# Loading and splitting the second up unit ahead of a norm chain, two small copies on another engine, and one head's transposes a matmul group sooner

## The chip, the cores and the metric

The kernel runs one decoder layer on 1 core of one Trainium2 chip. The metric is the device time of one execution in microseconds: 770.14 us, the median of three runs (770.01 to 772.16).

The core has five instruction streams. PE multiplies matrices into PSUM (PEld is its weight load). DVE (VectorE), ACT (ScalarE) and POOL (GpSimd) work on tiles, and SP (SyncE) only issues transfers; ACT issues transfers too, between its own instructions. Each stream runs in its own order, and an instruction that waits holds up everything behind it on its stream.

## The reference

One layer, 512 positions of width 1024, float32 throughout:

```python
mod = silu(c) @ ada_w + ada_b
sh1, sc1, g1, sh2, sc2, g2 = split(mod, 6)
u = rms_norm(x, mix_pre_g) * (1 + sc1) + sh1
qk, v, o_pre, gates, glu = split(u @ w_in)
h = mlstm(silu(conv4(qk)), v, gates)              # 4 heads of 256, chunks of 128
h = rms_norm(h, ml_norm_g) * sigmoid(o_pre)
y = silu(layer_norm(conv31(a * sigmoid(gt))))     # a, gt = halves of glu
x = x + g1 * rms_norm(concat(h, y) @ w_out, mix_post_g)
u = rms_norm(x, ffn_pre_g) * (1 + sc2) + sh2      # the "second norm"
a, gt = split(conv3(u @ ffn_up))                  # 2 x 2816 columns
x = x + g2 * rms_norm((silu(gt) * a) @ ffn_down, ffn_post_g)
```

## The kernel before

**Precision by splitting.** A large product is made of three fp32r passes. Each weight tile of 128x512 is split: ACT writes the rounded part `h` (`w_split`, L191), and DVE or POOL writes the rest `l` (L192). `mm3` (L210) multiplies h by h, h by l and l by h. A 1 MB weight load gives four such pairs, `_0`, `_512`, `_1024` and `_1536`. It lands in one of two raw buffers (pool `raws`), so a load can be issued only when the last split of the load before the previous one is done.

**Order.** PE and SP run in the order in which the code is written. DVE, ACT and POOL are ordered by a scheduler, except inside `in_order()`, where they too follow the written order. Transfers that ACT issues are placed among its instructions by the scheduler.

**Third head.** For heads 0 to 3, `attention(h)` is a generator that emits scores (`s`, L551), values (`o`, L562), the scaling of `hn` (L587) and last the transposes `hT` (L593) with their splits `hh` (ACT, L599) and `hl` (DVE, L600). While head 2 finishes, `make_vo(3)` emits four groups of 24 matmuls (`vo`), one for each 128 positions. The pair of PSUM banks tagged `at` holds `s`, `o`, `hT` and later `xT` in turn. After head 2, PE emits `ry_s` (L216), the sums of the convolution's layer norm, and head 3's first scores.

**The mixer's end and the second norm.** The output projection has two column halves. `mixa` is done first; `mixb` (four tiles of 128 positions) follows in two parts: eight row blocks for all tiles, then `mix_last(tt, ...)`, the other eight blocks tile by tile. As soon as `mixb` of a tile stands, its chain runs:

- `chain_sums`: square sum (ACT L717), `un = mixb * g1r` (DVE L968), factor `rm` (DVE L724, POOL L726);
- `chain_x`: the new residual `x1` (DVE L975), its square sums (ACT L717), `un = x1 * gs2r` (DVE L978), factor `rf`;
- `chain_u`: `un * rf + sh2r` (DVE L983);
- `turn_tile`: eight transposes on PE into `xT` (L991, the `at` banks); `turn_out`: the split into `u2h` (ACT L998) and `u2l` (DVE L999), which frees the banks.

`gs2r` and `sh2r` are rows spread over all partitions: DVE and ACT make `gains` (L948 to L950), PE transposes them (`gT`), DVE copies `gTs` (L694), SP sends that to DRAM (L696) and reads it back as four broadcasts (L702).

**Up units.** The first up unit (`wup0`) is loaded and split before the chain. Units 1 and 2 are loaded by `raw_up` (L1008) and split by `up_split`, four calls each, at places written into the chain. `up_half(th, i)` multiplies unit i with half of the positions; the first three units run in halves, so that PE starts on tiles 0 and 1 while tiles 2 and 3 are still in the chain. From unit 3 on, all positions are there. `x1` is stored to DRAM (`x1_d`) for the end of the layer.

Of the kernel before, what the change touches and what calls it, by code (L numbers as in the profile page):

```python
# [13 lines left out]
AF = mybir.ActivationFunctionType  # L14
ALU = mybir.AluOpType
# [5 lines left out]
KT = D // P  # L21
NT = T // P
# [33 lines left out]
def decoder_layer(ctx, tc, w_glu0, x, c, adaT, vecs, w_glu, w_qko, w_v0, w_vo, w_out, w_up, w_down, out):  # L56
    nc = tc.nc
    V, S, G, PE = nc.vector, nc.scalar, nc.gpsimd, nc.tensor

    const = ctx.enter_context(tc.tile_pool(name="const", bufs=1))  # L60
    slots = ctx.enter_context(tc.tile_pool(name="slots", bufs=SLOTS))
# [38 lines left out]
    def mmbank(name):  # L100
        return psum.tile([P, T], F32, tag="mm", bufs=4, name=name)

    def atbank(name):
        return psum.tile([P, T], F32, tag="at", bufs=2, name=name)
# [45 lines left out]
    def vcols(name, i, n):  # L150
        a = VEC[name][0] + i
        return vec[:, a : a + n]
# [32 lines left out]
    def w_split(src, name, pool=None, tag="w", eng=None):  # L185

        n = src.shape[1]
        pool = pool or wpool
        hi = pool.tile([P, T], F32R, tag=tag, name=f"{name}h")
        lo = pool.tile([P, T], F32R, tag=tag, name=f"{name}l")  # L190
        S.activation(hi[:, :n], src, AF.Copy)  # L191
        (eng or G).tensor_tensor(out=lo[:, :n], in0=src, in1=hi[:, :n].bitcast(F32), op=ALU.subtract)  # L192
        return hi, lo

    def w_load(view, name, pool=None, tag="w", eng=None):

        n = view.shape[1]
        r = raws.tile([P, 2048], F32, tag="raw", name=name)
        nc.sync.dma_start(r[:, :n], view)
        return [w_split(r[:, a : min(a + T, n)], f"{name}_{a}", pool, tag, eng) for a in range(0, n, T)]  # L200
# [37 lines left out]
    RD = float(D) ** 0.5  # L238
# [35 lines left out]
    for tt in range(NT):  # L274
# [9 lines left out]
        if tt < NT - 1:  # L284
# [7 lines left out]
                    op0=ALU.add)  # L292
# [9 lines left out]
    def u_tiles(name):  # L302
        hi = upool.tile([P, KT, T], F32R, tag="uh", name=f"{name}h")
        lo = upool.tile([P, KT, T], F32R, tag="ul", name=f"{name}l")
        return hi, lo, [(hi[:, j, :], lo[:, j, :]) for j in range(KT)]

    _, _, u = u_tiles("u")
# [211 lines left out]
    def head_load(h):  # L519
        pieces = []  # L520
        for part in range(2 if h else 3):
            pieces += w_load(w_qko[(2 * h + 1 if h else 0) + part], f"wqko{h}_{part}")
        heads[h] = (pieces, [], [], [])

    def head_proj(h, i):

        pieces, qs, ks, so = heads[h]
        ps = mmbank(f"qko{h}_{i}")
        proj(ps, pieces, i * KT)
        e = 2 * h + i % 2  # L530
        if i < 2:
            qs.append(conv4(ps, e, f"q{h}_{i}"))
        elif i < 4:
            ks.append(conv4(ps, 8 + e, f"k{h}_{i}"))
        else:
            t = slot(f"so{h}_{i}")
            S.activation(t, ps, AF.Tanh, scale=0.5)
            so.append(t)
# [146 lines left out]
    RD = float(D) ** 0.5  # L685
    gains = const.tile([P, 4 * KT], F32, name="gains")
    rows_d = [dram.tile([D], F32, tag=f"row{i}", name=f"row_d{i}") for i in range(4)]

    def send_rows(a, n, queue=nc.scalar):

        ps = mmbank(f"gT{a}") if a == KT else atbank(f"gT{a}")
        PE.transpose(ps[:n, :P], gains[:, a : a + n], ident)
        t = (side if a == 3 * KT else slot)(f"gTs{a}")[:, :P]
        V.tensor_copy(t[:n, :], ps[:n, :P])  # L694
        for i in range(n // KT):
            queue.dma_start(rows_d[a // KT + i].rearrange("(j p) -> j p", p=P), t[i * KT : (i + 1) * KT, :])  # L696
# [13 lines left out]
    x1_d = [[dram.tile([P, T], F32, tag=f"x1d{tt}_{hf}", name=f"x1d{tt}_{hf}") for hf in range(2)] for tt in range(NT)]  # L710
# [23 lines left out]
    sc2 = mod[:, 24:40].rearrange("p (j two) -> p j two", two=2)  # L734
# [74 lines left out]
    def pace():  # L809
        tc.cur_priority += LATER  # L810
        next(paced, None)
        tc.cur_priority -= LATER
# [14 lines left out]
    def norm_sums():  # L827
        yr.append(colsum(ysq, T, "ry_s", cvbank))
# [14 lines left out]
    for h in range(H - 1):  # L843
        head_load(h + 1)
        steps = attention(h)
        if h == 0:
            head_proj(1, 0)
            next(steps)
            head_proj(1, 1)
            pace()  # L850
            next(steps)
            pace()
            head_proj(1, 2)
            pace()
            next(steps)
        else:
            next(steps)
            head_proj(h + 1, 0)
            pace()
            for _ in turns:  # L860
                pass
            head_proj(h + 1, 1)
            pace()
            next(steps)
            scaled = last_e[0]
            pace()
            head_proj(h + 1, 2)
            pace()
            next(steps)
        head_proj(h + 1, 3)  # L870
        values = make_vo(h + 1)
        pace()
        next(steps)
        pace()
        next(values)
        next(steps)
        pace()
        next(values)
        if h == 0:
            next(steps)  # L880
            pace()
        make_E(h + 1)
        if h == H - 2:
            norm_mean()
        next(values)
        next(values)
        if h < H - 2:
            turns = steps
        else:
            for _ in steps:  # L890
                pass
        if h == H - 2:
            norm_sums()

# [40 lines left out]
    x1 = side_parts("x1_0") + side_parts("x1_1")  # L935
    x1 = [x1[2 * tt : 2 * tt + 2] for tt in range(NT)]
# [9 lines left out]
        for tt, ps in enumerate(banks):  # L946
            mm3(ps, (hy[k][0][:, tok(tt)], hy[k][1][:, tok(tt)]), wo[n_ % 4], n_ == 0, False)
    V.scalar_tensor_tensor(out=gains[:, KT : 2 * KT], in0=sc2[:, :, 0], scalar=1.0, in1=vcols("ffn_pre_g", 0, KT), op0=ALU.add, op1=ALU.mult)  # L948
    S.activation(gains[:, 2 * KT : 3 * KT], sc2[:, :, 1], AF.Copy)
    S.activation(gains[:, KT : 2 * KT], gains[:, KT : 2 * KT], AF.Copy, scale=RD)  # L950
    wo = [w for g in range(KA // 4, 4) for w in wo_rows(1, g)]
    for tt in range(NT):
        for hf in range(2):
# [8 lines left out]
    def chain_sums(tt):  # L962

        ps = banks[tt]
        sq_sum(ps, msq[:, 2 * tt + 1 : 2 * tt + 2], f"mixb{tt}")
        un = adas.tile([P, D], F32, tag="ada", name=f"un{tt}")
        uns[tt] = [un[:, :T], un[:, T:]]
        V.tensor_tensor(out=uns[tt][1], in0=ps, in1=g1r[1], op=ALU.mult)  # L968
        return token_factor(msq[:, 2 * tt : 2 * tt + 2], f"rm{tt}")
# [31 lines left out]
    def mix_last(tt, a, b):  # L1001
        for n_, k in enumerate(MIX[KA:]):
            if a <= n_ < b:
                mm3(banks[tt], (hy[k][0][:, tok(tt)], hy[k][1][:, tok(tt)]), wo[n_], False, n_ == 2 * KT - KA - 1)

    def raw_up(i):
        r = raws.tile([P, 2048], F32, tag="raw", name=f"wup{i}")
        nc.sync.dma_start(r, w_up[i])  # L1008
        up_w[i] = []
        return r  # L1010

    def up_split(i, r, pool, tag):
        q = len(up_w[i])
        up_w[i].append(w_split(r[:, q * T : (q + 1) * T], f"wup{i}_{q * T}", pool, tag, V))
# [9 lines left out]
                mm3(ps[:, th * HT : (th + 1) * HT], blk(up_w[i], half * KT + k), (u2h[:, th, k, :], u2l[:, th, k, :]), k == 0, k == KT - 1)  # L1024

    up_w = {0: w_load(w_up[0], "wup0", slots, "t", V)}
    send_rows(KT, 2 * KT, nc.sync)
    gs2r = row(1, cvtile, "gs2", nc.sync)
    sh2r = row(2, cvtile, "sh2", nc.sync)
    raw1 = raw_up(1)  # L1030
    raw2 = raw_up(2)
    early += [[mmbank(f"up{i}_{half}") for half in range(2)] for i in range(2)]
    with in_order():
        for tt in range(3):
            mix_last(tt, 0, 2 * KT - KA)
        r = chain_sums(0)
        r = chain_x(0, r)
        up_split(1, raw1, slots, "t")
        chain_u(0, r)
        turn_tile(0)  # L1040
        mix_last(3, 0, 7)
        r = chain_sums(1)
        up_split(1, raw1, slots, "t")
        r = chain_x(1, r)
        up_split(1, raw1, slots, "t")
        chain_u(1, r)
        turn_out(0)
        turn_tile(1)
        mix_last(3, 7, 2 * KT - KA)
        r = chain_sums(2)  # L1050
        turn_out(1)
        r = chain_x(2, r)
        up_split(1, raw1, slots, "t")
        chain_u(2, r)
        up_half(0, 0)
        turn_tile(2)
        r = chain_sums(3)
        up_split(2, raw2, wpool, "w")
        r = chain_x(3, r)
        up_split(2, raw2, wpool, "w")  # L1060
        chain_u(3, r)
        up_half(0, 1)
        up_split(2, raw2, wpool, "w")
        early.append([cvbank(f"up2_{half}") for half in range(2)])
        up_half(0, 2, 0)
        turn_tile(3)
        turn_out(2)
        up_split(2, raw2, wpool, "w")
        turn_out(3)
    up_half(0, 2, 1)  # L1070
    for i in range(NE):
        up_half(1, i)
    for tt in range(NT):
        for hf in range(2):
            nc.scalar.dma_start(x1_d[tt][hf], x1[tt][hf])


    def halves(z):
# [293 lines left out]
```

## Time and profile before

| | before |
|---|---|
| median of three runs | 770.14 us |
| the profiled execution's own time | 771.9 us |
| its span, first to last instruction | 770.2 us |
| PE busy | 758.1 us, 98% |
| DVE / POOL / ACT busy | 575.3 / 522.8 / 407.4 us |
| HBM read / written | 126.59 / 20.07 MB |
| granted PE clock | full speed until the last 21 us |

Times within the trace are counted from the span's first instruction. A row of the timeline gives start, duration, engine, line, operation, the tile written and the tiles read, and, in brackets, how long the engine had been idle and what ended that. The last ends of merged matmul rows are modelled, so the distance from start to start says more than the duration: 128x512 matmuls follow each other at 0.23 us here.

### The profile page before, as it was taken

What the parts mean: (1) busy time and instruction counts of PE and PEld (TensorE: products, weight loads), DVE (VectorE), ACT (ScalarE), POOL (GpSimd) and SP (SyncE); (2) the same over time, 40 slices, a digit from 0 to 9 for tenths busy, and PEclk for the clock granted to TensorE, in tenths of its full rate; (3) what the DMA queues carried; (4) which work ended last, traced back from release to release, by engine and by line L of the source; (5) the groups of instructions that cost most, each with busy time, mean ns of one, the idle gap of its engine ahead of it and who ended that gap; (6) DMA issues with size and microseconds to landing.
All of it is one profiled execution on the core that took longest, in us unless ns stands there. A gap on an engine that the chain in (4) does not pass through costs nothing.

```text
span 770.2 us, 10269 instructions
## 1 busy us (share of the span) xinstructions
PE 758.1 (98%) x3552; PEld 629.9 (82%) x3552; DVE 575.3 (75%) x831; ACT 407.4 (53%) x780; POOL 522.8 (68%) x432
## 2 busy tenths in 40 slices
PE   8999999999999999999998999999999999999996
PEld 6888898878788788788887998888888888888885
DVE  6769999979889686577949798665776578754548
ACT  6685538585665555563334554434444345566633
POOL 4789849794594871645521467876988786699934
PEclk9999999999999999999999999999999999999999
DMA  8973214311131350656953655756586683896273
GB/s 315 365 266 134 86 56 149 125 55 55 55 114 52 110 212 8 246 191 200 371 188 108 251 181 207 283 214 240 193 300 222 224 296 145 316 398 243 95 235 148
DMA packets 40138, 147.34 MB, mean 191 GB/s; under 512 B 3827, under 2 KB 5267, under 8 KB 30485
## 3 DMA queue, kind: packets, MB, share of 16 engines
q1 hardware_dynamic: 26372, 94.50, 34.2%
q10 hardware_dynamic: 13712, 52.18, 18.8%
q8 instruction: 28, 0.46, 0.2%
q14 instruction: 26, 0.20, 0.1%
HBM read 126.59 MB, written 20.07 MB: 190 GB/s over the span
## 4 chain that ended last, share of the span: by engine, by line
PE 88%; DMA 5%; DVE 2%; issue 2%; POOL 1%; ACT 1%; SPq 0%; DVEq 0%; POOLq 0%; ACTq 0%
PE up L210 31%; PE qko L210 13%; PE dn L210 10%; PE vo L210 9%; PE glu L210 7%; PE mixa L210 6%; PE glu L350 4%; PE s L551 2%; PE o L562 2%; DMA wup<-in_w_up 2%; PE v L210 1%; DMA p<-spill_t 1%; PE mixb L210 1%; DMA wglu<-in_w_glu 1%; DMA xn<-in_x 1%
## 5 line engine op out<-in xcount | busy, mean ns | idle before, releaser
L774 DVE SCALAR_TENSOR_TENSOR cv<-gt,cvw,cv 128x485 f32<-128x485 f32 (+24 forms) x200 | 137.1, 730 | 2.1 <-ACT cv L762 0.8
L770 POOL TENSOR_TENSOR cs<-cs,cs 128x510 f32<-128x510 f32 (+3 forms) x32 | 42.1, 1316 | 0.4 <-ACT cs L768 0.3
L210 PE MATMUL up<-u2h,wup_0h 128*128 128x512 f32 (+1 forms) x100 | 36.5, 365 | 0.0
L210 PE MATMUL up<-u2l,wup_0h 128*128 128x512 f32 (+1 forms) x100 | 36.5, 365 | 0.0
L210 PE MATMUL up<-u2h,wup_1024h 128*128 128x512 f32 (+1 forms) x100 | 36.4, 364 | 0.0
L210 PE MATMUL up<-u2h,wup_0l 128*128 128x512 f32 (+1 forms) x100 | 36.4, 364 | 0.0
L210 PE MATMUL up<-u2h,wup_1536l 128*128 128x512 f32 (+1 forms) x100 | 36.4, 364 | 0.0
L210 PE MATMUL up<-u2h,wup_512h 128*128 128x512 f32 (+1 forms) x100 | 36.4, 364 | 0.0
L210 PE MATMUL up<-u2l,wup_512h 128*128 128x512 f32 (+1 forms) x100 | 36.4, 364 | 0.0
L210 PE MATMUL up<-u2h,wup_512l 128*128 128x512 f32 (+1 forms) x100 | 36.4, 364 | 0.0
L210 PE MATMUL up<-u2h,wup_1536h 128*128 128x512 f32 (+1 forms) x100 | 36.4, 364 | 0.0
L210 PE MATMUL up<-u2l,wup_1536h 128*128 128x512 f32 (+1 forms) x100 | 36.4, 364 | 0.0
L210 PE MATMUL up<-u2h,wup_1024l 128*128 128x512 f32 (+1 forms) x100 | 36.4, 364 | 0.0
L210 PE MATMUL up<-u2l,wup_1024h 128*128 128x512 f32 (+1 forms) x100 | 36.3, 363 | 0.0
L176 DVE SCALAR_TENSOR_TENSOR junk<-ada,cb 128x1024 bf16<-128x1024 f32 x20 | 31.8, 1588 | 5.5 <-DMA ada<-in_adaT 5.3
L192 POOL TENSOR_TENSOR wup_0l<-wup,wup_0h 128x512 fp32r<-128x512 f32 x19 | 29.3, 1542 | 4.5 <-ACT wup_0h L191 4.5
L192 POOL TENSOR_TENSOR wup_1024l<-wup,wup_1024h 128x512 fp32r<-128x512 f32 x19 | 25.0, 1318 | 9.4 <-ACT wup_1024h L191 9.4
L192 POOL TENSOR_TENSOR wup_1536l<-wup,wup_1536h 128x512 fp32r<-128x512 f32 x19 | 27.2, 1430 | 4.8 <-ACT wup_1536h L191 4.5
L768 ACT ACTIVATE cs<-gt,cvw 128x511 f32<-128x511 f32 (+4 forms) x40 | 27.1, 713 | 6.0 <-POOL cs L770 3.5
L1105 POOL TENSOR_TENSOR b<-b 128x512 f32<-128x512 f32 x11 | 14.6, 1331 | 18.6 <-PE up L210 10.6
L1106 DVE TENSOR_TENSOR b<-b 128x512 f32<-128x512 f32 x11 | 19.4, 1761 | 10.1 <-POOL b L1105 10.1
L192 POOL TENSOR_TENSOR wup_512l<-wup,wup_512h 128x512 fp32r<-128x512 f32 x19 | 25.2, 1324 | 0.0
(1097 smaller groups left out, 2730.8 us busy)
## 6 DMA issues: line engine op xcount, KB each, us to landing
wup<-in_w_up SPq DMA_DIRECT2D x22, 1024.0 KB, 6.0
b<-in_w_down ACTq DMA_DIRECT2D x11, 1024.0 KB, 5.5
spill_t<-b ACTq DMA_DIRECT2D x11, 1024.0 KB, 4.2
ada<-in_adaT ACTq DMA_DIRECT2D x20, 512.0 KB, 4.2
wqko<-in_w_qko SPq DMA_DIRECT2D x9, 1024.0 KB, 4.8
ada<-in_adaT SPq DMA_DIRECT2D x16, 512.0 KB, 7.0
wo<-in_w_out SPq DMA_DIRECT2D x8, 1024.0 KB, 4.8
wvo<-in_w_vo SPq DMA_DIRECT2D x6, 1024.0 KB, 4.7
```

The costliest lines, as they stand in the source:

```text
L176: t = V.scalar_tensor_tensor(out=junk, in0=r, scalar=1.0, in1=cb, op0=ALU.mult, op1=ALU.mult, accum_out=mod[:, i : i + 1])
L192: (eng or G).tensor_tensor(out=lo[:, :n], in0=src, in1=hi[:, :n].bitcast(F32), op=ALU.subtract)
L210: PE.matmul(ps, l, r, start=start and i == 0, stop=stop and i == 2, skip_group_check=again)
L350: PE.matmul(ps, blk(wk, i)[a], u[k][b], start=k == 0 and p == 0, stop=k == KT - 1 and p == 1)
L551: PE.matmul(sp[:, :n], ks[d][:, cc * P : (cc + 1) * P], qs[d][:, cc * P :], start=d == 0, stop=d == 1)
L562: PE.matmul(o[:, : DH + 2], E[h][cc][:, a : a + P], vs[h][cc], start=cc == 0, stop=cc == tt)
L768: S.activation(t[:, d:], cvx[j][:, : T - d], AF.Copy, scale=w(CK - 1 - d))
L770: G.tensor_tensor(out=side[:, d:], in0=side[:, d:], in1=t[:, d:], op=ALU.add)
L774: tap = V.scalar_tensor_tensor(out=cp[:, d:], in0=cvx[j][:, : T - d], scalar=w(CK - 1 - d), in1=cp[:, d:], op0=ALU.mult, op1=ALU.add)
L1105: G.tensor_tensor(out=b12, in0=b22, in1=b12, op=ALU.subtract)
L1106: V.tensor_tensor(out=b22, in0=b22, in1=b11, op=ALU.subtract)
```

## The change

1. The third head's transposes and splits come after three `vo` groups of the fourth head instead of four: the last `next(values)` stands behind the rest of `attention(2)`.
2. Two of the three small `gains` operations (128x8) go from ACT to DVE.
3. `raw_up(1)` is issued in front of the scale rows, and its four splits are written in front of `chain_sums(0)` instead of among the chains of tiles 0, 1 and 2.
4. `raw_up(2)` is issued behind `chain_x(0)`, and the stores of `x1` go from ACT's queue to SP's: tile 0's before `raw_up(2)`, the other three tiles' after it and before unit 3's load.

```diff
@@ -883,12 +883,12 @@
         next(values)
-        next(values)
         if h < H - 2:
             turns = steps
         else:
             for _ in steps:
                 pass
+        next(values)
         if h == H - 2:
             norm_sums()
@@ -946,8 +946,8 @@
-    S.activation(gains[:, 2 * KT : 3 * KT], sc2[:, :, 1], AF.Copy)
-    S.activation(gains[:, KT : 2 * KT], gains[:, KT : 2 * KT], AF.Copy, scale=RD)
+    V.tensor_copy(gains[:, 2 * KT : 3 * KT], sc2[:, :, 1])
+    V.tensor_scalar(out=gains[:, KT : 2 * KT], in0=gains[:, KT : 2 * KT], scalar1=RD, scalar2=None, op0=ALU.mult)
@@ -1024,25 +1024,30 @@
     up_w = {0: w_load(w_up[0], "wup0", slots, "t", V)}
+    raw1 = raw_up(1)
     send_rows(KT, 2 * KT, nc.sync)
     gs2r = row(1, cvtile, "gs2", nc.sync)
     sh2r = row(2, cvtile, "sh2", nc.sync)
-    raw1 = raw_up(1)
-    raw2 = raw_up(2)
+
+    def x1_store(tt):
+        for hf in range(2):
+            nc.sync.dma_start(x1_d[tt][hf], x1[tt][hf])
+
     with in_order():
         for tt in range(3):
             mix_last(tt, 0, 2 * KT - KA)
+        for _ in range(4):
+            up_split(1, raw1, slots, "t")
         r = chain_sums(0)
         r = chain_x(0, r)
-        up_split(1, raw1, slots, "t")
+        x1_store(0)
+        raw2 = raw_up(2)
         chain_u(0, r)
         turn_tile(0)
         mix_last(3, 0, 7)
         r = chain_sums(1)
-        up_split(1, raw1, slots, "t")
         r = chain_x(1, r)
-        up_split(1, raw1, slots, "t")
         chain_u(1, r)
 ...
         r = chain_x(2, r)
-        up_split(1, raw1, slots, "t")
         chain_u(2, r)
 ...
-    for tt in range(NT):
-        for hf in range(2):
-            nc.scalar.dma_start(x1_d[tt][hf], x1[tt][hf])
+    for tt in range(1, NT):
+        x1_store(tt)
```

How the order moves, first on PE around the third head's transposes (`hT`; `vo_2` and `vo_3` are the third and fourth `vo` group). Before:

```order
L210 MATMUL vo_3_3001<-wvo_1_1536h,ul 128x512
L593 MATMUL hT_0_3028<-ident,hn_0_2775 128x128 x2
L593 MATMUL hT_0_3028<-ident,hn_1_2776 128x128 x2
L593 MATMUL hT_1_3037<-ident,hn_0_2775 128x128 x2
L593 MATMUL hT_1_3037<-ident,hn_1_2776 128x128 x2
L216 MATMUL ry_s<-ones,ysq 128x1 x4
L551 MATMUL s_0_3067<-q_0c,k_2c 128x512
```

Now the transposes stand between the third and the fourth group:

```order
L210 MATMUL vo_2_2974<-wvo_1_1536h,ul 128x512
L593 MATMUL hT_0_3001<-ident,hn_0_2775 128x128 x2
L593 MATMUL hT_0_3001<-ident,hn_1_2776 128x128 x2
L593 MATMUL hT_1_3010<-ident,hn_0_2775 128x128 x2
L593 MATMUL hT_1_3010<-ident,hn_1_2776 128x128 x2
L210 MATMUL vo_3_3019<-wvo_0_0h,uh 128x512
```

Between the transposes and the scores `s_0` there are now 24 matmuls more; `ry_s` and `s_0` follow `vo_3` as before.

On SP, from the first up unit's load on (`row_d` are the scale rows' sends, `x1d` the stores; `wup_3786` and `wup_3772` are unit 1, `wup_3788` and `wup_3903` unit 2, `wup_4422` unit 3). Before:

```order
L199 DMA wup_3754<-in_w_up 128x2048
L696 DMA row_d_1416<-gTs_3774 8x128
L696 DMA row_d_1417<-gTs_3774 8x128
L702 DMA gs2r_3778<-row_d_1416 128x512
L702 DMA gs2r_3779<-row_d_1416 128x512
L702 DMA sh2r_3782<-row_d_1417 128x512
L702 DMA sh2r_3783<-row_d_1417 128x512
L1008 DMA wup_3786<-in_w_up 128x2048
L1008 DMA wup_3788<-in_w_up 128x2048
L199 DMA wup_4422<-in_w_up 128x2048
```

And now, from the last of the scale rows on (unit 1's load `wup_3772` and the other five scale-row transfers stand ahead of these rows, in that order):

```order
L702 DMA sh2r_3785<-row_d_1417 128x512
L1034 DMA x1d_0_1419<-x_0_3552 128x512
L1034 DMA x1d_1_1420<-x_0_3552 128x512
L1008 DMA wup_3903<-in_w_up 128x2048
L1034 DMA x1d_0_1421<-x_0_3552 128x512
L1034 DMA x1d_1_1422<-x_0_3552 128x512
L1034 DMA x1d_0_1423<-x_1_3553 128x512
L1034 DMA x1d_1_1424<-x_1_3553 128x512
L1034 DMA x1d_0_1425<-x_1_3553 128x512
L1034 DMA x1d_1_1426<-x_1_3553 128x512
L199 DMA wup_4422<-in_w_up 128x2048
```

Unit 1's load went ahead of all six scale-row transfers, directly behind unit 0's; unit 2's is behind two stores, unit 3's behind eight.

On DVE, around the start of tile 0's chain (`un_3882` is its first tile; `wup_3772` is unit 1). Now:

```order
L948 SCALAR_TENSOR_TENSOR gains<-mod,vec 128x8
L949 COPY gains<-mod 128x8
L950 TENSOR_SCALAR gains<-gains 128x8
L192 TENSOR_TENSOR wup_0l<-wup_3754,wup_0h 128x512
L192 TENSOR_TENSOR wup_512l<-wup_3754,wup_512h 128x512
L192 TENSOR_TENSOR wup_1024l<-wup_3754,wup_1024h 128x512
L192 TENSOR_TENSOR wup_1536l<-wup_3754,wup_1536h 128x512
L694 COPY gTs_3776<-gT_3774 16x128
L192 TENSOR_TENSOR wup_0l<-wup_3772,wup_0h 128x512
L192 TENSOR_TENSOR wup_512l<-wup_3772,wup_512h 128x512
L192 TENSOR_TENSOR wup_1024l<-wup_3772,wup_1024h 128x512
L192 TENSOR_TENSOR wup_1536l<-wup_3772,wup_1536h 128x512
```

The next row is tile 0's L968. Before, unit 1's four splits were not here: the first stood between L724 and L983 of tile 0, the second and third in tile 1's chain, the fourth in tile 2's. ACT's four halves (L191) moved the same way, ahead of tile 0's square sum, and the two `gains` rows left ACT, where they stood between two splits of the last `w_out` load.

## The prediction

> **What bounds the kernel now.** I read the page, then PE's waits, then the chain that ended last.
>
> ```profile
> PE 758.1 (98%) x3552; PEld 629.9 (82%) x3552; DVE 575.3 (75%) x831; ACT 407.4 (53%) x780; POOL 522.8 (68%) x432
> ```
>
> ```profile
> PE xT L991 <- DVE u2l L999: 1.4, 1, 1.4
> PE xT L991 <- DVE un L968: 0.6, 1, 0.6
> ...
> PE s L551 <- DVE hl L600: 0.4, 1, 0.4
> ```
>
> ```profile
> 431.90 205.13 PE up L210 x984
> ...
> 637.14 21.81 PE up L210 x96
> 658.95 73.68 PE dn L210 x324
> ```
>
> PE is the bound. Between the start and the tail it waits three times, and these are the three places that the change touches. Behind 431.90 the chain stays on PE for 300 us, so a microsecond that PE gains earlier reaches the end, unless something there runs by its own clock.
>
> **Part 1, the transposes one group sooner.**
>
> ```profile
> 310.60 1.03 PE L593 MATMUL hT<-ident,hn 128*128 128x128 f32 x8
> 311.47 0.95 PE L216 MATMUL ry_s<-ones,ysq 128*128 128x1 f32 x8
> 312.87 0.70 PE L551 MATMUL s<-q_0c,k_2c 128*128 128x512 f32 x1 [0.45 <-DVE hl L600]
> ```
>
> ```profile
> 296.84 1.38 DVE L587 TENSOR_SCALAR hn<-hn,fac,rd 128x256 f32<-128x256 f32 x4 [1.54 <-POOL fac L579]
> ...
> 302.47 0.36 ACT L650 ACTIVATE E<-Mb,ga 128x128 f32<-128x128 f32 x1
> ...
> 305.35 0.39 ACT L501 ACTIVATE v<-vo 128x256 f32<-128x256 f32 x1 [1.71 <-PE vo L210]
> ```
>
> The scores need the bank that `hl` frees. From 311.47 the eight `ry_s` rows at about 0.11 us would end at 312.35; the scores start at 312.87 and their first matmul takes about 0.1 more than its three sisters: 0.6 to 0.7 lost. Sooner, the transposes stand at 305.2, where `vo_2` ends: `hn` is ready since 298.2, their banks since 302.8, and behind them `hh` and `hl` have 24 matmuls (5.45 us) instead of 0.9. So the wait goes. The price is one change more from transposes to fp32r:
>
> ```profile
> 350.69 0.47 PE L210 MATMUL mixa<-wo_1024h,yh 128*128 128x512 f32 x1
> 351.01 0.39 PE L210 MATMUL mixa<-wo_1024l,yh 128*128 128x512 f32 x1
> ```
>
> 0.32 instead of 0.23: 0.09. ACT now takes both `hh` ahead of six splits of `w_out`, about 1.3 us later each, and POOL's `ry_r` with them; that is covered by 5 us, and uncovered it would cost those 1.3. Term: -0.6, bounds 0 and -0.7.
>
> **Part 2, the copies on VectorE.**
>
> ```profile
> 381.56 2.27 POOL L192 TENSOR_TENSOR wo_512l<-wo,wo_512h 128x512 fp32r<-128x512 f32 x1
> ...
> 386.18 1.29 POOL L192 TENSOR_TENSOR wo_1024l<-wo,wo_1024h 128x512 fp32r<-128x512 f32 x1 [2.35 <-ACT wo_1024h L191]
> 387.43 1.75 POOL L192 TENSOR_TENSOR wo_1536l<-wo,wo_1536h 128x512 fp32r<-128x512 f32 x1
> ```
>
> ```profile
> ACT gains L949 <- DVE mod L181: 6.3, 1, 6.3
> ```
>
> ACT stood 6.3 us before `gains` while two splits of `w_out` were queued behind it. Without it POOL goes on at 383.8, and unit 1's raw buffer, free at 389.2 before, is free between 386.4 (two splits at 1.29) and 389.2; I take 387, since POOL shares its stretch with DVE until 385. The two operations on DVE, 0.2 each at most by its other 128x8 rows, lie in the 2.0 us that DVE waits for unit 0's first split. By itself: 0.
>
> **Part 3, unit 1 ahead of the scale rows and of the chain.**
>
> ```profile
> 394.30 0.86 SPq L1008 DMA_DIRECT2D wup<-in_w_up  x2
> ```
>
> ```profile
> 399.96 0.55 POOL L726 TENSOR_TENSOR rf0r<-rf0t,mhalf 128x1 f32<-128x1 f32 x1 [2.91 <-DVE rf0t L724]
> ...
> 403.35 0.63 ACT L191 ACTIVATE wup_0h<-wup 128x512 fp32r<-128x512 f32 x1 [3.71 <-DMA wup<-in_w_up]
> ...
> 404.01 0.69 DVE L192 TENSOR_TENSOR wup_0l<-wup,wup_0h 128x512 fp32r<-128x512 f32 x1 [4.13 <-ACT wup_0h L191]
> 404.62 1.41 DVE L983 SCALAR_TENSOR_TENSOR un<-un,rf0r,sh2r 128x512 f32<-128x512 f32 x2
> ```
>
> ```profile
> 405.52 0.60 PE L991 MATMUL xT<-ident,un 128*128 128x128 f32 x4
> 406.69 0.66 PE L991 MATMUL xT<-ident,un 128*128 128x128 f32 x4 [0.57 <-DVE un L968]
> ...
> 411.73 0.39 PE L210 MATMUL mixb<-wo_1024h,yl 128*128 128x512 f32 x1
> 413.55 1.26 PE L991 MATMUL xT<-ident,un 128*128 128x128 f32 x8 [1.43 <-DVE u2l L999]
> ```
>
> Unit 1 was issued at 394.30, behind the scale rows, and was there at 403.3. Its first split stood in tile 0's chain, so DVE was idle for 4.1 us although the factor `rf0r` stood at 400.5. Everything behind is late by that: tile 0's second four transposes start 1.17 behind the first (0.44 at 0.11 each, so 0.73 lost), tile 1's start 1.82 behind a matmul that gives way after 0.23 (1.59 lost). Sum: 2.32.
>
> Now unit 1 is issued at 387. When it lands:
>
> ```profile
> 386.00:392.40 6.40, 6.40 (x31) 5.17 (x30) 3.82 (x5) 2.81 (x6) 3.00 (x2) 1.00 0.01 1
> ```
>
> ```profile
> DMA to landing us min/median/max: 4.7/6.6/11.6
> ```
>
> The transfer engines are idle there (share 0.01), so of the 4.7 to 11.6 us that unit loads took I take the least: 391.7. ACT's and DVE's four splits then end 3.2 later, at 394.9. The chain before began at 395.6 and begins 0.6 sooner now, at 395.0:
>
> ```profile
> 395.61 0.69 DVE L968 TENSOR_TENSOR un<-mixb,g1r 128x512 f32<-128x512 f32 x1 [4.49 <-ACT mixb0junk L717]
> ...
> 405.94 0.69 DVE L968 TENSOR_TENSOR un<-mixb,g1r 128x512 f32<-128x512 f32 x1
> ...
> 411.49 1.41 DVE L983 SCALAR_TENSOR_TENSOR un<-un,rf1r,sh2r 128x512 f32<-128x512 f32 x2
> ...
> 412.81 1.28 DVE L999 TENSOR_TENSOR u2l<-xT,u2h 128x512 fp32r<-128x512 f32 x2
> ```
>
> So it isn't held. `un` of tile 0 ends at 401.4, and PE asks at 404.9. Tile 1's L968 moves from 405.94 to 401.4; from there to `un`'s end it was 7.0 us, less 0.6 for the two splits that left: 407.8. `u2l` of tile 0 frees the banks at 409.1; PE, now without its first stall, asks at 410.6. Both stalls go, with 1.5 us to spare. What is late next is `turn_out(1)`: from the transposes to the first `up` matmul with `u2l` it is 2.07 us (413.55 to 415.62), ACT's and DVE's own time, and stays. Tile 2 is the tight one:
>
> ```profile
> 419.78 1.41 DVE L983 SCALAR_TENSOR_TENSOR un<-un,rf2r,sh2r 128x512 f32<-128x512 f32 x2
> ...
> 421.36 1.04 PE L991 MATMUL xT<-ident,un 128*128 128x128 f32 x8
> ```
>
> 0.17 us in hand, counted from tile 1's transposes on both sides; the split that leaves this chain adds 0.3. Term: -2.35, bounds 0 and -2.6 (the 0.26 between 415.34 and 415.62 too).
>
> **Part 4, the stores on SP.** ACT loses eight issues, which delayed only square sums that DVE's L978 covers: 0. On SP, unit 3's load now waits for tile 3's `x1`.
>
> ```profile
> 419.89 90.05 SPq L199 DMA_DIRECT2D wup<-in_w_up  x9
> ```
>
> ```profile
> 423.61 0.75 DVE L975 SCALAR_TENSOR_TENSOR x<-un,rm3r,x 128x512 f32<-128x512 f32 x1
> ...
> 431.50 1.09 ACT L998 ACTIVATE u2h<-xT 128x512 fp32r<-128x512 f32 x2 [1.41 <-PE xT L991]
> ...
> 434.60 0.28 PE L210 MATMUL up<-u2h,wup_0h 128*128 128x256 f32 x1
> ```
>
> `x1` was done at 424.4 and will be at 421.2, so unit 3 goes out at 421.7 instead of 419.9. On ACT two of its splits stand ahead of tile 3's `u2h`, which PE needs about 1.3 us before 431.8 (434.60 less the gain and 0.1). So unit 3 must land by 429.3, 7.6 us after its issue. Behind 0.5 MB of stores I take 5 to 6 us, with the median of 6.6 still inside: 0. The Trainium skill, "DMA: Bandwidth & Descriptors", section "Queues, rings and completion order", speaks against this part: the transfers of one issuing engine are taken in turn from one ring, and the transfer engines alternate only between the rings of different issuers, so stores on SP's ring stand wholly in front of the load, where on ACT's they would share. The trace agrees as far as it goes: unit 1 behind four scale rows took 9.0 us. The sum would be the same by it, only the rival below likelier.
>
> **Sum.** The profiled execution took 771.9 us (span 770.2): 771.9 - 0.6 - 2.35 = 768.95. The median of the runs is 1.76 below it: 770.14 - 2.95 = 767.2.
>
> **Rivals.**
>
> - *Unit 1 lands late.* Its splits now stand ahead of the whole chain on ACT and DVE, where before only 4 us stood behind them. Up to a landing at 393.2 (1.5 us to spare) nothing is lost, from there each microsecond costs one, first at tile 1's transposes. With the buffer free only at 389.2 it lands at 393.9: 767.9. At 396.2 the gain is gone, and at 11.6 us after issue (398.6) it is 767.2 + 5.4 = 772.6, slower than before. For: the page shows loads of 7 us and more. Against: the idle transfer engines. 0.14, a third of it slower.
> - *Unit 3 lands late* behind the stores: from 429.3 on one for one, at most 11.6 us after issue, 433.3: 767.2 + 4 = 771.2. 0.07.
> - *The gain is given back.* A bank, a load or the modulation blocks that DVE reads between the first `up` units keep their time, and PE meets them 3 us sooner; tile 2 with its 0.17 is the first candidate. A part comes back, 768.2 to 769.6. Against: not one wait on PE in 300 us. 0.13.
> - *The head's part does nothing* or costs, because the splits of `w_out` are later: 767.9. Inside the forecast's range.
>
> **How the numbers follow.** Forecast 0.66, with its own range 766.6 to 768.0 (bounds of the two terms, and some tenths of noise). 0.3%, about what a measurement of this kernel can tell from no change, is 2.3 us: faster means below 767.8. Most of the forecast and a little of the rivals lie there: 0.63; slower than 772.45 needs a very late unit 1 or what I haven't seen: 0.07; the rest 0.30. For eight in ten I go from 766.3 to 770.0.
>
> **What would show it.** Right: PE's waits on `xT` and on `s` are gone; unit 1's load starts near 387 and lands before 393; DVE's L968 of tile 0 starts near 395 and never waits for a split of unit 1; the first `up` matmul of unit 0 starts near 412.5. Wrong: DVE waiting for `wup_0h` ahead of L968; ACT waiting for unit 3 ahead of `u2h`; PE waiting at tile 2's transposes; or all waits gone and PE's start of `dn`, 658.95 before, not near 656.

## The result

The changed kernel takes 769.34 us, the median of 22 runs (768.52 to 771.32); the kernel before, run beside it, takes 770.92 us (769.64 to 773.18). The ratio is 0.9983, with a 95% interval of 0.9975 to 0.9991: about 1.3 us less (0.7 to 1.9; the two medians are 1.58 apart), which is under half of the 2.95 us that the prediction summed, and within the 0.3% that it called no change.

In the profiled execution the change did what was forecast, place by place. The page of the changed kernel, and PE's waits between 300 and 420 us, all of them:

```profile
PE 757.2 (99%) x3552; PEld 628.8 (82%) x3552; DVE 576.6 (75%) x833; ACT 406.8 (53%) x778; POOL 525.8 (68%) x432
```

```profile
PE up L210 <- DVE u2l L999: 0.2, 1, 0.2
```

The waits on `s` and on `xT` are gone. What is left is the first `up` matmul's wait for `u2l`, of 0.2 us. The timeline of the same execution, in order of time (SP's, ACT's, DVE's and PE's rows together):

```profile
144.46 0.41 PE L676 MATMUL mtok<-ident,Mr 4*128 4x4 f32 x4
...
305.66 1.03 PE L593 MATMUL hT<-ident,hn 128*128 128x128 f32 x8
311.99 0.95 PE L216 MATMUL ry_s<-ones,ysq 128*128 128x1 f32 x8
312.80 1.10 PE L551 MATMUL s<-q_0c,k_2c 128*128 128x512 f32 x2
...
386.26 0.33 SPq L1008 DMA_DIRECT2D wup<-in_w_up  x1
391.14 0.63 ACT L191 ACTIVATE wup_0h<-wup 128x512 fp32r<-128x512 f32 x1 [3.54 <-DMA wup<-in_w_up]
393.62 0.69 DVE L192 TENSOR_TENSOR wup_1536l<-wup,wup_1536h 128x512 fp32r<-128x512 f32 x1
395.51 0.69 DVE L968 TENSOR_TENSOR un<-mixb,g1r 128x512 f32<-128x512 f32 x1 [1.20 <-ACT mixb0junk L717]
405.42 1.03 PE L991 MATMUL xT<-ident,un 128*128 128x128 f32 x8
411.08 1.03 PE L991 MATMUL xT<-ident,un 128*128 128x128 f32 x8
```

Unit 1 is issued at 386.26 (forecast 387) and there at 391.1 (391.7). Its last split ends at 394.3 (394.9), and the chain that follows waits for ACT's square sum and not for a split. All sixteen transposes run without a gap.

To compare the middle of the kernel across executions I count from a fixed point, the first row of the 4x4 transposes `mtok` (L676), which both kernels have and which stands ahead of all that the change touches. In the profile of before it is this row of the timeline:

```profile
143.96 0.41 PE L676 MATMUL mtok<-ident,Mr 4*128 4x4 f32 x4
```

And the chain of waits of the changed kernel has the start of `dn`:

```profile
656.41 102.24 PE dn L210 x450
```

From `mtok` to `dn` it was 514.99 us (143.96 to 658.95) and is 511.95: 3.04 us less, where the sum had 2.95. So the profile confirms the prediction and the clock does not: 3.0 us in one pair of executions, 1.3 us by the ratio of all runs. The experiments ask where the other 1.7 us are.

### The profile page after: what moved, and what is told of

The parts are those of the page before. It is cut to its first block, busy times and chain, and to the rows that moved or that the text cites. A ratio compares the mean times of both kernels' runs of the same rounds, so it can differ in the third digit from the quotient of the medians.

```text
span 767.6 us, 10277 instructions
## 1 busy us (share of the span) xinstructions
PE 757.2 (99%) x3552; PEld 628.8 (82%) x3552; DVE 576.6 (75%) x833; ACT 406.8 (53%) x778; POOL 525.8 (68%) x432
## 4 chain that ended last, share of the span: by engine, by line
PE 97%; DMA 1%; issue 0%; ACT 0%; DVEq 0%; SPq 0%; DVE 0%; POOLq 0%; POOL 0%; ACTq 0%
PE up L210 31%; PE dn L210 13%; PE qko L210 13%; PE vo L210 9%; PE glu L210 7%; PE mixa L210 6%; PE mixb L210 6%; PE glu L350 4%; PE o L562 2%; PE s L551 2%; PE v L210 2%; DMA wglu<-in_w_glu 1%; DMA xn<-in_x 1%; PE hT L593 0%; PE xT L991 0%
## 5 line engine op out<-in xcount | busy, mean ns | idle before, releaser
L330 DVE SCALAR_TENSOR_TENSOR junk<-ada,cps 128x1024 bf16<-128x1024 f32 x16 | 19.5, 1219 | 8.5 <-DMA ada<-in_adaT 7.8
```

The lines of the kernel that those rows point to most:

```text
L330: V.scalar_tensor_tensor(out=junk, in0=first[k][:, i * D : (i + 1) * D], scalar=1.0, in1=cps, op0=ALU.mult, op1=ALU.mult, accum_out=part[: ...
```

## The experiments

Two theories were set against each other. **A:** the waits at `xT` are not a property of the kernel but of the execution; the profiled one had long ones, a common one has less to gain. **B:** the waits are there every time, and the changed kernel gives part of the gain back somewhere that its one profile does not show.

### Both kernels once more

No edit.

> The kernel before, unchanged, as a second profile of it. The profiled execution of before lost 2.9 us in three waits of PE (0.6 ahead of s, 0.73 and 1.59 ahead of xT), and the changed kernel has none of them, yet the medians differ by 1.3 to 1.6 us only. Theory A, the waits vary from execution to execution with the landing of unit 1 (403.3 in the profile): this profile lands unit 1 sooner, at 399 to 402, its waits at xT sum to 0.5 to 1.5 us instead of 2.3, and its time is near 770.5. Theory B, the waits are fixed and the missing part is given back elsewhere (start of the kernel, tail, clock): the waits at xT sum to 2.2 to 2.4 again and unit 1 lands within 0.5 us of 403.3. Against before both expect a ratio of 1.000.

> The changed kernel, unchanged, as a second profile of it beside the others on the same chip. Ratio 0.9983 again (0.9975 to 0.9991). Theory A: no PE wait at s or xT in this profile either, unit 1 landed near 391, and from the first transposes of the third head to the start of dn the time agrees within 0.2 us with the first profile of it. Theory B, the gain is given back in some executions of the changed kernel: a wait at xT or at the split of unit 1 or 3 stands in this profile, 0.5 us or more.

Before against itself: 1.0002 (0.9992 to 1.0012). The changed kernel: 0.9983 (0.9973 to 0.9993), a second time. In its second profile the time is 769.41 us, unit 1's first split on ACT starts at 391.00 and PE has the same single wait of 0.2 us. That takes away B's first form, a wait that comes in some executions of the changed kernel: from `mtok` to the last matmul the two profiles agree within 0.1 us. The second profile of before, PE's and ACT's rows of the timeline:

```profile
144.15 0.41 PE L676 MATMUL mtok<-ident,Mr 4*128 4x4 f32 x4
...
402.80 0.63 ACT L191 ACTIVATE wup_0h<-wup 128x512 fp32r<-128x512 f32 x1 [2.91 <-DMA wup<-in_w_up]
405.69 1.11 PE L991 MATMUL xT<-ident,un 128*128 128x128 f32 x8
413.01 1.25 PE L991 MATMUL xT<-ident,un 128*128 128x128 f32 x8 [1.41 <-DVE u2l L999]
```

Tile 0's eight transposes now run through; the wait of 0.73 us among them is not there. Tile 1's still is: its transposes start 1.80 us behind the matmul ahead of them, 1.57 over the pitch of 0.23. Unit 1's first split on ACT, which waits for the landing, starts 0.55 us sooner than before's 403.35. One wait of three is already a matter of the execution. But 1.57 is more than A's 1.5 and less than B's 2.2, so this decides nothing.

### Each half by itself

The head alone, on the kernel before:

```diff
         next(values)
-        next(values)
         if h < H - 2:
             turns = steps
         else:
             for _ in steps:
                 pass
+        next(values)
```

> Before with the third head's transposes one group sooner and nothing else. The wait ahead of s goes. By the prediction: -0.6 us, ratio 0.9992. Theory A: the same -0.6, since this wait depends on no transfer. Rival, PE gives the time back at the waits for xT, since the chain there is tied to transfers that do not move (unit 1 lands at its own time): between 0 and -0.2 us, ratio 0.9998 to 1.000, with the waits for xT grown by up to 0.6.

Ratio 0.9992 (0.9981 to 1.0003). The interval holds the forecast of -0.6 us and the rival's 0 as well, so the clock does not decide between them. In the profile the wait at `s` is gone. Its rows at `xT`, and from its chain of waits the start of `dn`:

```profile
145.77 0.41 PE L676 MATMUL mtok<-ident,Mr 4*128 4x4 f32 x4
...
403.29 0.63 ACT L191 ACTIVATE wup_0h<-wup 128x512 fp32r<-128x512 f32 x1 [2.43 <-DMA wup<-in_w_up]
406.74 1.03 PE L991 MATMUL xT<-ident,un 128*128 128x128 f32 x8
413.50 1.25 PE L991 MATMUL xT<-ident,un 128*128 128x128 f32 x8 [0.93 <-DVE u2l L999]
...
658.90 90.00 PE dn L210 x396
```

This execution had a slow start (`mtok` 1.8 us later than in the first profile), unit 1 came at the same time as there (403.29 against 403.35), and the wait at `xT` is 1.09 us instead of 2.33. It is what PE has left to wait when it arrives.

And here the rival is what happened. The third profile of the kernel before, shown below, has unit 1's first split at the same distance behind `mtok` as this one: 257.52 us (403.29 - 145.77, and 401.64 - 144.12). From `mtok` to `dn` both take 513.13 us (658.90 - 145.77, and 657.25 - 144.12). With the edit PE comes to `xT` 0.6 us sooner and waits there 1.09 us instead of 0.47. So the 0.6 us are given back where unit 1 is late; they reach the end only where PE has no wait at `xT` to run into.

Unit 1 alone, load and splits, on the kernel before:

```diff
     up_w = {0: w_load(w_up[0], "wup0", slots, "t", V)}
+    raw1 = raw_up(1)
...
-    raw1 = raw_up(1)
     raw2 = raw_up(2)
...
+        for _ in range(4):
+            up_split(1, raw1, slots, "t")
         r = chain_sums(0)
         r = chain_x(0, r)
-        up_split(1, raw1, slots, "t")
         chain_u(0, r)
...
         r = chain_sums(1)
-        up_split(1, raw1, slots, "t")
         r = chain_x(1, r)
-        up_split(1, raw1, slots, "t")
...
         r = chain_x(2, r)
-        up_split(1, raw1, slots, "t")
```

> Before with unit 1's load ahead of the scale rows and its four splits ahead of tile 0's chain; unit 2's load behind the rows as before, the stores on ACT's queue and the small copies on ACT. Prediction: raw buffer free at 389.2, unit 1 issued then and landed near 393.9 to 394.5, DVE's first L968 0.5 to 2 us later than 395.6, both waits at xT gone or under 0.7 in all: -1.6 to -2.3 us, ratio 0.9970 to 0.9979. Theory A (typical waits at xT of 0.5 to 1.5 us): -0.3 to -1.2 us, ratio 0.9984 to 0.9996. Theory B: -1.6 to -2.3.

Ratio 0.9992 (0.9983 to 1.0000): -0.6 us, theory A's price, and B's -1.6 lies outside the interval. Its profile has no wait at `xT`; unit 1 is there at 393.4. From `mtok` to `dn` it takes 512.56 us (656.65 - 144.09); with the head's edit added, in the last run of this section, 511.94 (656.78 - 144.84). Behind an early unit 1 the head's edit is thus worth 0.62 us in full. The two halves as timed, 0.6 us each, add up to the 1.3 us of the whole, but the head's half is known no better than its interval, and by the profiles it depends on the other.

### Work put into the waits

Ten matmuls more on PE, on either kernel, ahead of the last `mixb` blocks:

```diff
     with in_order():
+        for _ in range(10):
+            PE.matmul(early[0][0], hy[MIX[0]][0][:, tok(0)], wo[0][0], start=True, stop=True)
         for tt in range(3):
             mix_last(tt, 0, 2 * KT - KA)
```

> Before with ten matmuls of 128x512 more on PE (2.27 us at 0.227 each, into a bank that is overwritten later) behind gT and ahead of mix_last(0), so 10 to 17 us ahead of the waits at xT. Unit 1's chain does not pass through them. What the waits hold is filled by these matmuls first, so the time that they cost is 2.27 us less the waits that a common execution has. Theory A (waits at xT of 0.5 to 1.5 us in a common execution, more in an execution whose start was quick): +0.8 to +1.8 us, ratio 1.0010 to 1.0023. Theory B (2.3 us of waits in every execution, the gain of the change lost elsewhere): +0.0 to +0.3 us, ratio 1.0000 to 1.0004.

> The changed kernel with the same ten matmuls. It has no wait at xT to fill: both theories +2.27 us less at most 0.3 (the first wait of the up matmuls for u2l), ratio against before 0.9983 + 0.0027 = 1.0010 to 1.0012. If it costs clearly less, PE still has a wait that the profiles do not show.

Before with the matmuls: 1.0022 (1.0013 to 1.0030), +1.7 us (1.0 to 2.3). Of the 2.27 us that they take on PE only about 0.6 went into waits. This is the measurement that does not rest on a profile: in a common execution of before there are 0.6 us (0 to 1.3) to be had at `xT`, not 2.3. Theory B asked for 1.0000 to 1.0004, and falls.

The changed kernel with them: 1.0020 (1.0006 to 1.0033), +2.9 us against the unpadded one by the two ratios. The interval holds the 1.0010 to 1.0012 that both theories gave and is too wide to say more. In the profiles the price from `mtok` to `dn` is 2.25 us on the kernel before (660.25 - 145.43 = 514.82, against the 512.57 of the fourth profile below, which has no wait at `xT` either) and 2.51 on the changed kernel (659.90 - 145.44 = 514.46, against 511.95). The 0.25 us more are a wait that is new: the load of up unit 3 behind the stores came into view. SP's issue of unit 3, the split on ACT that waits for it, and tile 3's last `u2h` behind that:

```profile
425.21 0.46 SPq L199 DMA_DIRECT2D wup<-in_w_up  x1
...
433.16 0.63 ACT L191 ACTIVATE wup_0h<-wup 128x512 fp32r<-128x512 f32 x1 [4.95 <-DMA wup<-in_w_up]
...
435.22 0.59 ACT L998 ACTIVATE u2h<-xT 128x512 fp32r<-128x512 f32 x1
```

8.0 us from issue to first split, and PE's first two `up` matmuls of the second half lost 0.25 us against their pitch there. In the changed kernel itself the same rows of the timeline are:

```profile
421.96 1.04 SPq L199 DMA_DIRECT2D wup<-in_w_up  x1
...
428.80 0.63 ACT L191 ACTIVATE wup_0h<-wup 128x512 fp32r<-128x512 f32 x1 [3.83 <-DMA wup<-in_w_up]
```

6.8 us. The prediction's limit for this split, 429.3, counts in the profile of before; with `mtok` 0.50 us later it is 429.8 here, and the split starts 1.0 us inside it. With the ten matmuls the limit is 433.05 (1.48 for `mtok`, 2.27 for the matmuls), and the split starts 0.1 us behind it.

### The kernel before, twice more

What decides the size of the waits: when PE arrives, or when unit 1 lands?

> The kernel before as a third profile. Theory A in its sharper form: tile 1's transposes start when unit 1's splits let them, at 412.5 to 413.8 in every profile of before, however late PE comes there; PE comes there 267.2 us after its first 4x4 transposes (mtok), which stand at 144.0 to 145.8 by how quick the start of the execution was. So the waits at xT sum to the difference: 1.5 to 2.3 us where mtok is near 144, 0 to 0.9 where it is near 145.5. Theory B (waits of a fixed length): 1.6 to 2.4 with either.

> The kernel before as a fourth profile, with the same expectation as the third: by theory A the waits at xT sum to the time of release (412.5 to 413.8) less the first 4x4 transposes' time less 267.2; by theory B to 1.6 to 2.4 always.

Third profile, 770.31 us:

```profile
144.12 0.41 PE L676 MATMUL mtok<-ident,Mr 4*128 4x4 f32 x4
...
401.64 0.63 ACT L191 ACTIVATE wup_0h<-wup 128x512 fp32r<-128x512 f32 x1 [1.68 <-DMA wup<-in_w_up]
405.71 1.03 PE L991 MATMUL xT<-ident,un 128*128 128x128 f32 x8
411.85 1.25 PE L991 MATMUL xT<-ident,un 128*128 128x128 f32 x8 [0.31 <-DVE u2l L999]
...
657.25 73.68 PE dn L210 x324
```

Fourth, 769.34 us:

```profile
143.84 0.41 PE L676 MATMUL mtok<-ident,Mr 4*128 4x4 f32 x4
...
400.45 0.63 ACT L191 ACTIVATE wup_0h<-wup 128x512 fp32r<-128x512 f32 x1 [0.90 <-DMA wup<-in_w_up]
405.42 1.03 PE L991 MATMUL xT<-ident,un 128*128 128x128 f32 x8
411.08 1.03 PE L991 MATMUL xT<-ident,un 128*128 128x128 f32 x8
```

Both miss the expectation. It had the release of tile 1's transposes fixed at 412.5 to 413.8, and so 1.5 to 2.3 us of waits where `mtok` is near 144. With `mtok` at 144.12 and 143.84 the waits were 0.47 us and none at all. The sharper form of A is wrong: the landing is not fixed. A itself stands, and the profiles now give its law. L is the start of unit 1's first split on ACT, M that of `mtok`:

| profile | M | L | waits at `xT` | L - M - 257.06 |
|---|---|---|---|---|
| before, first | 143.96 | 403.35 | 2.33 | 2.33 |
| before, second | 144.15 | 402.80 | 1.57 | 1.59 |
| before, third | 144.12 | 401.64 | 0.47 | 0.46 |
| before, fourth | 143.84 | 400.45 | 0.00 | -0.45 |
| head alone (PE 0.61 sooner behind M) | 145.77 | 403.29 | 1.09 | 0.46 + 0.61 = 1.07 |
| before with ten matmuls (2.27 later) | 145.43 | 403.80 | 0.00 | 1.31 - 2.27 = -0.96 |

The constant 257.06 is fitted to the first three rows; the other three test it. One for one, within 0.02 us, the wait is what unit 1's landing is late against PE, and nothing below zero. And the whole time follows: the profiled execution's time less M less the wait is 625.6, 625.6, 625.7 and 625.5 us in the four profiles of before, and 624.9 in both of the changed kernel (769.35 - 144.46 and 769.41 - 144.53). So the whole change is worth about 0.7 us in each of these executions, and the wait on top, between 0 and 2.3. The fourth execution of before took 769.34 us, as much as the changed kernel's median, but with the earliest `mtok` of all. One profile falls out of this sum: the head alone has 625.4 (772.27 - 145.77 - 1.09), because behind `dn` it took 113.37 us where the others took 112.9 to 113.1. Why was not traced.

### Which part of the unit 1 edit does it

Only the load moved, on the kernel before; the splits stay among the chains:

```diff
     up_w = {0: w_load(w_up[0], "wup0", slots, "t", V)}
+    raw1 = raw_up(1)
...
-    raw1 = raw_up(1)
     raw2 = raw_up(2)
```

> Before with unit 1's load ahead of the scale rows and nothing else: its four splits stay where they were, one in tile 0's chain, two in tile 1's, one in tile 2's. Issue near 389, landing near 394. Theory A (it was the landing alone that held the chain): DVE does not wait for wup_0h behind L978, both waits at xT are gone (under 0.3 in all), ratio 0.9992 as with load and splits moved together. Rival, the splits' place matters too (0.6 us of DVE each ahead of un): PE still waits 0.5 to 1.5 us at tile 1's transposes, ratio 0.9995 to 1.000.

Ratio 0.9990 (0.9980 to 0.9999). PE does not wait at `xT` in the profile, and the first split stands where it stood, in the chain, without having waited for data. DVE's row of the timeline:

```profile
400.97 0.69 DVE L192 TENSOR_TENSOR wup_0l<-wup,wup_0h 128x512 fp32r<-128x512 f32 x1 [0.31 <-ACT wup_0h L191]
```

The 0.31 us is ACT's own split. From `mtok` to `dn` it takes 512.55 us (657.29 - 144.74), with the splits moved too 512.56. The earlier issue is enough; where the four splits are written makes no difference that shows.

### The price of a late load behind the new splits

The changed kernel with unit 1's load behind the scale rows again:

```diff
     up_w = {0: w_load(w_up[0], "wup0", slots, "t", V)}
-    raw1 = raw_up(1)
     send_rows(KT, 2 * KT, nc.sync)
     gs2r = row(1, cvtile, "gs2", nc.sync)
     sh2r = row(2, cvtile, "sh2", nc.sync)
+    raw1 = raw_up(1)
```

> The changed kernel with unit 1's load put back behind the scale rows; its splits stay ahead of tile 0's chain. It prices the rival of the prediction: from a landing at 393.2 each microsecond costs one. Issue near 392.6, landing 8 to 9 us later near 401, the chain of tile 0 held until 404.2: +7.8 us against the changed kernel, ratio against before near 1.0085 (1.006 to 1.010), with DVE waiting for wup_0h ahead of L968 and PE waiting at tile 0's transposes, where it had come to at 405.4. Rival, the waits ahead of tiles 1 and 2 add to it: over 1.010. Rival, nothing is held, because the splits have slack: 0.998.

Ratio 1.0070 (1.0055 to 1.0086), slower than before, and 6.7 us over the changed kernel by the two ratios. The profiled execution, 778.38 us, is the slowest of its six (from 774.65). Its timeline, with the load's issue, ACT's and DVE's first work on it, tile 0's chain, and PE:

```profile
395.34 0.38 SPq L1008 DMA_DIRECT2D wup<-in_w_up  x1
403.49 0.63 ACT L191 ACTIVATE wup_0h<-wup 128x512 fp32r<-128x512 f32 x1 [12.48 <-DMA wup<-in_w_up]
404.15 0.69 DVE L192 TENSOR_TENSOR wup_0l<-wup,wup_0h 128x512 fp32r<-128x512 f32 x1 [11.98 <-ACT wup_0h L191]
406.57 0.68 DVE L968 TENSOR_TENSOR un<-mixb,g1r 128x512 f32<-128x512 f32 x1
412.24 2.38 PE L991 MATMUL xT<-ident,un 128*128 128x128 f32 x8 [5.61 <-DVE un L983]
```

DVE stands for 12 us and the whole chain behind it. The same landing, 403.4, cost before 2.3 us with one split in the chain, and costs 8.0 us here (from `mtok` to `dn` 519.95 against 511.95). The splits ahead of the chain bring nothing by themselves and make the kernel sensitive to the load; it is the load's new place that makes this safe. If each microsecond of lateness costs one, nothing is lost up to a first split 249.99 us behind `mtok` (403.49 - 8.0 - 145.50); in the changed kernel it stands at 246.68 (391.14 - 144.46), 3.3 us inside.

### Copies and stores

The copies back on ACT, in the changed kernel:

```diff
-    V.tensor_copy(gains[:, 2 * KT : 3 * KT], sc2[:, :, 1])
-    V.tensor_scalar(out=gains[:, KT : 2 * KT], in0=gains[:, KT : 2 * KT], scalar1=RD, scalar2=None, op0=ALU.mult)
+    S.activation(gains[:, 2 * KT : 3 * KT], sc2[:, :, 1], AF.Copy)
+    S.activation(gains[:, KT : 2 * KT], gains[:, KT : 2 * KT], AF.Copy, scale=RD)
```

> The changed kernel with the two small copies back on ACT. Prediction: unit 1's raw buffer comes free near 388 to 389 instead of 386.3, unit 1 lands near 393 to 394, DVE's first L968 starts near 396.4 instead of 395.5, and PE does not wait at xT: 0.0 us, ratio 0.9983 like the changed kernel. Rival, the later landing reaches PE: up to +0.8 us, ratio 0.9993.

Ratio 0.9987 (0.9978 to 0.9996), not to be told from 0.9983. Unit 1 is issued at 389.29, 3.0 us later than in the changed kernel; 1.2 of these are the later start of this execution (`mtok` at 145.65 against 144.46), 1.8 the copies. ACT's row is

```profile
394.04 0.63 ACT L191 ACTIVATE wup_0h<-wup 128x512 fp32r<-128x512 f32 x1 [5.15 <-DMA wup<-in_w_up]
```

and PE has no wait at `xT`. The copies buy 1.8 us of slack for the load and no time.

Last, the head and unit 1 (the edits of the two halves together), without the copies and without the stores on SP; of the loads' order only this moves:

```diff
         next(values)
-        next(values)
...
+        next(values)
...
     up_w = {0: w_load(w_up[0], "wup0", slots, "t", V)}
+    raw1 = raw_up(1)
...
-    raw1 = raw_up(1)
     raw2 = raw_up(2)
...
+        for _ in range(4):
+            up_split(1, raw1, slots, "t")
         r = chain_sums(0)
```

> Before with the head's transposes one group sooner, unit 1's load ahead of the scale rows and its splits ahead of the chain, without the small copies on DVE and without the stores on SP. By the prediction (both left-out parts cost or bring nothing) the whole of the change: ratio 0.9983 (0.9978 to 0.9990), no wait of PE at s or xT. Rival, the stores' new place or the copies bring something: 0.9988 or more.

Ratio 0.9980 (0.9971 to 0.9990). These two edits are the whole of the change as far as the clock can tell. This kernel and the one with the copies back on ACT differ by part 4 alone, the place of the stores and of unit 2's load: 0.9980 and 0.9987, with intervals that overlap, and 511.94 against 511.96 us (657.61 - 145.65) from `mtok` to `dn`. So part 4 by itself shows no effect on PE.

## Why the prediction was right in its steps and wrong in its size

**What failed** is part 3's term, -2.35, and with it the step that carries the sum from the profiled execution to the median: "770.14 - 2.95 = 767.2". The mechanism is right, and for the profiled execution so is the size, 2.33. But that wait belongs to the execution. In a common one it is 0.6 us (0 to 1.3), by the ten matmuls and by unit 1 alone; the four profiles average 1.1, and the term's lower bound, 0, is the fourth of them. The prediction treated the 1.76 us between the profiled execution and the median as something that both kernels keep. In good part they were this very wait: against before's fourth profile the first took 2.56 us more, of which 2.33 are the waits at `xT` and 0.12 a later start. To take the waits out and then subtract the excess again counts them twice. What stands in its place: about 0.7 us in every execution, and 0.6 at `xT` in a common one. Together 1.3 us.

The base was off as well. 770.14 is the median of three runs, and 22 runs give 770.92. So the forecast of 767.2 missed 769.34 by 0.8 us through its base and by 1.4 us through the gain (2.95 against the 1.58 between the medians).

No rival said that the wait might be small in other executions, though the profile had the warning: loads of one size took 4.7 to 11.6 us to land, and a wait that is the end of such a load is as uncertain as the load. That the range 766.3 to 770.0 held 769.34 is luck: it reached that far for other rivals, and most of the chance lay on faster by over 0.3%, which did not come.

**Part 1's term,** -0.6 for a wait on no transfer, held within the whole change: the wait at `s` is in all four profiles of before and in none with the edit, and the constant part of the time fell by 0.7 us. What the sum does not say is that the two terms hang together. With unit 1 late, the head's 0.6 goes into the wait at `xT`, as in the profile of the head alone; it needs part 3, or an execution in which unit 1 is not late, to reach the end. The timed ratio of this edit, 0.9992, is not by itself clear of 1.

**Parts 2 and 4** were costed at nothing, and nothing is what the runs show. The raw buffer came free at 386.3, just ahead of its 386.4 to 389.2. Unit 3's load, for which part 4 took 5 to 6 us, took 6.8 and in the second profile 6.5 (428.57 - 422.03), inside the 7.6 that it allowed.

**Rivals.** *Unit 1 late* didn't come, and its price is right in kind: 8.0 us for a landing at 403.5. By the prediction's rule (one for one from 393.2, moved by the 1.54 us that `mtok` is later than in before's profile) it would have been 8.75, so there was 0.75 us more slack than I had worked out. *Unit 3 late* came near: 1.0 us of slack, and 0.25 us lost in the profile with ten matmuls, where the load took 8.0 us. The page of the Trainium skill that spoke against this part ("DMA: Bandwidth & Descriptors", "Queues, rings and completion order") points the same way, but no run here has the same load with and without stores ahead of it at one place: the one pair that differs by part 4 alone also issues unit 3 some 27 us apart (396.08 and 423.17). *The gain given back* was the rival that the medians suggest, and it is not what happened: from `mtok` to `dn` the changed kernel keeps all of it, in both profiles. What is given back is the head's part alone, on the kernel before.

## What to carry to other kernels

A wait on PE that goes back to a transfer's landing is here a draw, not a constant: price it from several executions, or fill it with work of a known length and time that, before it enters a sum. Where the profiled execution is slower than the median, ask first whether the very wait that is to be removed is the reason. Two waits in a row on one engine need not be two separate terms: what is gained at the first can go into the second. And moving a load forward was worth as much as moving the load and its users; with the users in front of the chain and the load left where it was, the kernel is 0.7% slower than before.

## What the runs showed of the hardware

The same load at the same place of the same kernel took 7.3 to 9.1 us from its issue to its first use, and the four executions issued it between 393.17 and 395.12 us. First and fourth profile of before, SP's rows:

```profile
379.39 0.33 SPq L199 DMA_DIRECT2D wup<-in_w_up  x1
...
394.30 0.86 SPq L1008 DMA_DIRECT2D wup<-in_w_up  x2
```

```profile
378.29 0.33 SPq L199 DMA_DIRECT2D wup<-in_w_up  x1
...
393.17 0.86 SPq L1008 DMA_DIRECT2D wup<-in_w_up  x2
```

1.1 us of the 2.9 us by which L differs between the two were there at unit 0's issue already, the rest came on the way: 9.05 against 7.28 us from unit 1's issue to its first split. Issued ahead of the scale rows, the same load took 4.7 to 5.0 us in the six profiles whose first split waits for it (391.14 - 386.26 = 4.88 in the changed kernel). The start of the kernel varies likewise: `mtok` stood between 143.84 and 145.77 us in the fourteen profiles, whatever was changed behind it. What sets either was not traced further.
